# One reciprocal root per token, spread by TensorE; remainders of more weight tiles by the adding DMA; one room each for the mix buffers

## The chip, the cores and the metric

The kernel runs on one core of one Trainium2 chip. Its time is the device time of one launch in microseconds (us). The parts of the core named below are TensorE (PE, which multiplies a stationary 128x128 operand with a moving one into a PSUM bank), VectorE (DVE), ScalarE (ACT), GpSimd (POOL) and the sync engine's queue (SP), which issues the plain DMAs. PEld is the load of PE's stationary operand. POOL issues the DMAs that add to what stands in SBUF.

## The reference

Two layers, each with three residual steps on h, which is 512 tokens x 1024 in fp32:

```python
u = rms_norm(h, g_mlp) @ w_ff1                       # 1024 -> 4096
h = h + jnp.square(jax.nn.relu(u)) @ w_ff2           # 4096 -> 1024
gate = jax.nn.sigmoid(rms_norm(h, g_ple) @ w_ple_gate + b_ple_gate)
h = h + gate * (p_i @ w_ple)
```

In front of these stands h + [sparse attention heads || mLSTM heads](rms_norm(h) @ w_in) @ w_out, called the mix below. rms_norm(x, g) is x * rsqrt(mean(x*x) + 1e-6) * g. The reciprocal root is one number per token, so it can be applied after a matrix product.

## The kernel before

h is held transposed: eight tiles `const_1` to `const_8`, each 128 features (partitions) x 512 tokens. So the token runs along the free dimension, and a factor per token must lie in all 128 partitions as a row of 512.

All products are exact to fp32: an operand x is split into `hi` (x rounded to fp32r by an ACT copy) and `lo` (x - hi), and a product is three matmuls (`mm3`): hi*hi, lo*hi, hi*lo. A weight tile (`weight`, line 541 ff.) is 128x1024: a raw load by SP (`raw<-ws`), the ACT copy `hi`, and `lo` in one of two ways. The direct way is one DVE subtraction `lo<-raw,hi`. The adder way (adder=True) is a second ACT copy, of -hi into `lo`, and a DMA issued by POOL that adds the raw tile to it (`lo<-raw`); the raw tile must then stay until that DMA has landed.

`prep` makes the split operands of a norm: for each of the eight tiles of h, ACT squares it, POOL adds the square to a running sum (`acc`), and ACT and DVE make hi and lo of h times the gain. `wide_r` (lines 612-628) then turns `acc` (128x512) into the reciprocal root of each token, in all partitions: an ACT copy, a DVE subtraction, two matmuls 128x512 with a matrix of ones (sum over partitions, tile `ps_tr`), a DVE scale (`s<-ps_tr`), and ten DVE operations of `rsqrt` on 128x512. It is called twice in a layer: in the MLP (lines 1237-1240) and in the gate step, called ple (line 1311). The mix has its own forms: `token_r` (four matmuls 128x1, then rsqrt on 128x4, a token to a partition) and `spread` (lines 630-649), which lays such a 128x4 out as 128x512 by two diagonal tiles and two matmuls with ones.

The MLP has 32 tiles of w_ff1 and 32 of w_ff2 in a layer. The first four of w_ff1 are direct (`ff1`, lines 1252-1256). The other 28 go in 14 pairs (`pair`, `left`, lines 771-801 and 815 ff.) by Strassen's scheme with seven products of 256 columns. `left` loads two raw tiles r1 and r2, and DVE builds from them r3 (the tile `sum`), r1-r2 and so on, in place; ACT and DVE split each. A product adds into PSUM bank x, and DVE or ACT must read x before the next product adds to it. Between the products of a pair stand blocks of w_ff2, whose tiles are adder tiles; so per pair SP loads r1, r2 and two adder tiles. After the MLP the ple step multiplies two tiles of w_ple, then eight tiles of w_ple_gate, all direct.

The order of the work is made by a planner (`Plan`, list scheduling in Python with ranks and costs) and then pinned: each engine's queue is issued in that order, and every recorded operation bears line L390. Buffers live in rooms (line 1338): `s` 62 (128x512), `raw` 4, `sum` 1, `hi` 4, `lo` 4 and so on. A buffer waits until the last user of its room is done, and SP issues in order, so a load that waits for a room holds up those behind it.

Of the kernel before, what the change touches and what calls it, by code (L numbers as in the profile page):

```python
# [401 lines left out]
class Trunk:  # L402
# [209 lines left out]
    def wide_r(self, acc, dim):  # L612

        nc = self.nc
        chain, nc.chain = nc.chain, None
        label, nc.label = nc.label, "norm"
        hi, lo = self.slot([128, S], F32R), self.slot([128, S], F32R)
        nc.scalar.activation(hi, acc, AF.Copy)
        nc.vector.tensor_tensor(lo, acc, hi.bitcast(F32), op=ALU.subtract)
        ps = self.psum("tr")  # L620
        nc.tensor.matmul(ps, self.onesr, hi, start=True, stop=False)
        nc.tensor.matmul(ps, self.onesr, lo, start=False, stop=True)
        nc.chain = chain
        v = self.slot([128, S])
        nc.vector.tensor_scalar(v, ps, 1.0 / dim, EPS, op0=ALU.mult, op1=ALU.add)
        r = self.rsqrt(v, [128, S])
        nc.label = label
        return r

# [112 lines left out]
    def operands(self, xs, forms):  # L742

        H = S // 2
        lower, upper = slice(0, H), slice(H, S)
        out = []
        for j, (t12, t34) in enumerate(forms):
            d, first = {}, self.slot([128, S], F32R)  # L750
# [33 lines left out]
    def left(self, l, i):  # L784
# [5 lines left out]
        r3 = self.slot([128, 1024], F32, "sum")  # L790
# [70 lines left out]
    def mix(self, l):  # L861
# [42 lines left out]
        at = [self.slot([128, GA]) for _ in range(NTB)]  # L904
# [8 lines left out]
        for tb in range(NTB):  # L913
            nc.scalar.activation(at[tb], pss[tb][:, 0:GA], AF.Copy, scale=r[:, tb:tb + 1])
        ks = [at[tb][:, 0:192].split(64) for tb in range(NTB)]
        wi = self.tiny([128, NTB, 8])
        for tb in range(1, NTB):
            nc.vector.tensor_scalar(wi[:, tb], at[tb][:, 320:328], IDX_SCALE, None, op0=ALU.mult)
# [62 lines left out]

        gi, gf = g4(), g4()
        for tb in range(NTB):
            nc.vector.tensor_tensor(gi[:, tb], at[tb][:, 328:332], ct[:, T_I:T_I + 4], op=ALU.add)
            nc.vector.tensor_tensor(gf[:, tb], at[tb][:, 332:336], ct[:, T_F:T_F + 4], op=ALU.add)
# [46 lines left out]
        vx = [self.slot([128, 4, 129]) for _ in range(NTB)]  # L1032
        for tb in range(NTB):
            nc.gpsimd.memset(vx[tb][:, :, 128:129], 1.0)
        rh = self.tiny([128, NTB])
        nc.vector.tensor_scalar(rh, r, 0.5, None, op0=ALU.mult)
        og = []
        for base in (W_V, W_O):
            ps = [self.psum("proj") for _ in range(NTB)]
            for k in range(KD):  # L1040
                if k % 2 == 0:
                    w = self.wtile(l, base + k // 2, adder=True)
                for tb in range(NTB):
                    self.token_step(ps[tb], w, 512, xs[k], k, 2, tb, k == 0, k == KD - 1)
            for tb in range(NTB):
                if base == W_V:
                    nc.scalar.activation(vx[tb][:, :, 0:128], ps[tb].split(128), AF.Copy, scale=r[:, tb:tb + 1])
                else:
                    og.append(self.slot([128, 512]))
                    nc.scalar.activation(og[tb], ps[tb], AF.Tanh, scale=rh[:, tb:tb + 1])  # L1050
# [23 lines left out]
        for qb in range(NTB):  # L1074
# [3 lines left out]
            for h in range(8):  # L1078
# [21 lines left out]
                for sb in range(qb + 1):  # L1100
                    nc.tensor.matmul(po[:, h * 64:(h + 1) * 64], et[:, sb * 128:(sb + 1) * 128],
                                     at[sb][:, 192 + g * 64:256 + g * 64], start=sb == 0, stop=sb == qb)
# [18 lines left out]
        for h in range(4):  # L1121
# [26 lines left out]
            for tb in range(NTB):  # L1148
                for sb in range(tb + 1):
                    c = (tb - sb) * 128  # L1150
                    nc.tensor.matmul(where(tb), ptile[sb][:, c:c + 128], vx[sb][:, h], start=sb == 0, stop=sb == tb)
# [71 lines left out]
    def mlp(self, l):  # L1223
# [28 lines left out]
        def ff1(i, n=1):  # L1252
            for j, ps in enumerate(self.blocks([self.wtile(l, W_FF1 + i + j) for j in range(n)], xs)):
# [41 lines left out]
    def ple(self, l):  # L1295
# [7 lines left out]
        for n0, cnt in ((0, 2), (2, 1), (3, 1), (4, 1), (5, 1), (6, 1), (7, 1)):  # L1303
            ws = [self.wtile(l, W_GATE + n0 + j) for j in range(cnt)]

            last = l == L - 1 and n0 == KD - 1
            for c in (slice(0, S // 2), slice(S // 2, S)) if last else (slice(0, S),):
                pss = self.blocks(ws, [(hi[:, c], lo[:, c]) for hi, lo in xs], c)
                for n, ps in enumerate(pss, n0):
                    if rbc is None:  # L1310
                        rbc = self.wide_r(acc, D)
# [26 lines left out]
ROOMS = {"s": 62, "raw": 4, "sum": 1, "hi": 4, "lo": 4, "tiny": 48, "wide": 16, "m8": 4, "ps": 8}  # L1338
# [85 lines left out]
```

## Time and profile before

| | |
|---|---|
| median of three runs | 1372.84 us (1370.74 to 1373.17) |
| profiled execution | 1370.38 us, span 1368.7 us |
| granted TensorE clock, mean | 0.989 of full |
| busy: PE, PEld | 1320.8 us (97%), 1127.3 us (82%) |
| busy: DVE, ACT, POOL | 960.8 us (70%), 776.5 us (57%), 194.5 us (14%) |
| DMA | 176.37 MB, the 16 engines about half busy |

The span runs from the first to the last recorded instruction; the profiled execution's own time is 1.7 us more. In a row of the timeline the first number is the start in us from the span's start, the second how long the operation (or the run of like operations, xN) took, and the brackets hold the idle time of the engine before it with what ended it. Names of tiles have their numbers cut off in the profile: `s` is any tile of the s rooms, `const` here mostly h. The MLP of layer 0 runs from about 280 to 620 us, its ple step to 690; those of layer 1 from 955 and from 1295 us.

### The profile page before, as it was taken

Reading aid. Unit: us, or ns where it says so; the run is one execution under the profiler, and the core shown is the slowest. Engines: PE = TensorE matmul, PEld = TensorE weight load, DVE = VectorE, ACT = ScalarE, POOL = GpSimd, SP = SyncE. Lnnn points to the kernel's source line nnn. Section 1 sums busy time; section 2 is a strip of 40 time slices with the busy share of each in tenths; the row PEclk is TensorE's granted clock in tenths of the full one; section 3 lists DMA queues with packets and bytes.
Section 4 is the critical chain, followed back from the end, with each engine's and each line's share of the span. In section 5 each row is a group of like instructions: output and inputs, shape, how many; then the busy total and the mean of one; then the engine's idle time right before and its main releaser. Section 6 shows DMA issues by size and latency. Waiting matters only on the chain.

```text
span 1368.7 us, 20039 instructions
## 1 busy us (share of the span) xinstructions
PE 1320.8 (97%) x7344; PEld 1127.3 (82%) x7344; DVE 960.8 (70%) x2066; ACT 776.5 (57%) x1463; POOL 194.5 (14%) x233
## 2 busy tenths in 40 slices
PE   7999989989999999999999999999999999999988
PEld 6877868868988888987897778887888889889877
DVE  7899697596555656547859996957865565756484
ACT  4885685565545455455548956757554536445541
POOL 4221110210001010012113211003000101000110
PEclk9999999999999999999999999999999999999999
DMA  6556630535555555664243677024546555456621
GB/s 205 125 140 169 153 78 2 138 93 159 134 152 140 156 143 144 160 163 129 73 123 77 159 172 163 33 47 108 139 129 163 132 151 149 140 145 164 169 77 62
DMA packets 51075, 176.37 MB, mean 129 GB/s; under 512 B 6048, under 2 KB 6560, under 8 KB 50976
## 3 DMA queue, kind: packets, MB, share of 16 engines
q1 hardware_dynamic: 34848, 116.37, 26.2%
q0 software_dynamic: 16128, 58.73, 23.2%
q8 instruction: 57, 0.93, 0.3%
q14 instruction: 42, 0.34, 0.1%
HBM read 114.25 MB, written 2.10 MB: 85 GB/s over the span
## 4 chain that ended last, share of the span: by engine, by line
PE 60%; DMA 14%; DVE 13%; issue 9%; ACT 3%; SPq 0%; POOL 0%; POOLq 0%; DVEq 0%; ACTq 0%
PE ps_proj L390 51%; DMA raw<-ws 8%; DVE s L390 5%; DMA lo<-raw 5%; PE ps_tr L390 3%; DVE lo L390 3%; PE ps_sc L390 2%; PE ps_po L390 2%; ACT s L390 1%; DVE const L390 1%; DVE tiny L390 1%; PE ps_pn L390 1%; DMA s<-pt 1%; DVE sum L390 1%; ACT hi L390 1%
## 5 line engine op out<-in xcount | busy, mean ns | idle before, releaser
L390 PE MATMUL ps_proj<-s,hi 128*128 128x256 f32 (+1 forms) x3408 | 889.3, 352 | 14.8 <-ACT s L390 5.7
L390 PEld LDWEIGHTS ps_proj<-s,hi 128*128 128x128 f32 x3408 | 594.6, 190 | 108.1 <-DVE s L390 8.2
L390 PE MATMUL ps_proj<-s,lo 128*128 128x256 f32 (+1 forms) x1704 | 593.6, 351 | 2.5 <-DVE lo L390 2.3
L390 PEld LDWEIGHTS ps_proj<-s,lo 128*128 128x128 f32 x1704 | 322.8, 189 | 49.7 <-DVE lo L390 4.9
L390 ACT ACTIVATE hi<-raw 128x1024 fp32r<-128x1024 f32 (+1 forms) x212 | 221.4, 1046 | 194.9 <-PE ps_proj L390 146.4
L390 POOL DMA_DIRECT2D lo<-raw x112 | 96.7, 864 | 907.2 <-ACT lo L390 593.3
L390 ACT ACTIVATE s<-s 128x512 fp32r<-128x512 f32 (+3 forms) x174 | 101.0, 601 | 130.2 <-DVE s L390 111.9
L390 DVE TENSOR_TENSOR const<-const,ps_proj 128x512 f32<-128x512 f32 x160 | 109.3, 683 | 73.7 <-PE ps_proj L390 73.3
L390 DVE TENSOR_TENSOR lo<-raw,hi 128x1024 fp32r<-128x1024 f32 (+1 forms) x99 | 125.3, 1269 | 21.1 <-ACT hi L390 11.9
L390 DVE TENSOR_TENSOR s<-s,s 128x512 fp32r<-128x512 f32 (+2 forms) x140 | 98.7, 727 | 40.7 <-ACT s L390 39.2
L390 ACT ACTIVATE lo<-raw 128x1024 fp32r<-128x1024 f32 x112 | 117.8, 1052 | 11.9 <-PE ps_proj L390 7.7
L390 PE MATMUL ps_proj<-hi,s 128*128 128x512 f32 (+1 forms) x384 | 112.0, 380 | 7.9 <-ACT hi L390 7.1
L390 DVE TENSOR_TENSOR sum<-raw 128x512 f32<-128x512 f32 x28 | 19.4, 692 | 135.9 <-DMA raw<-ws 135.9
L390 PE MATMUL ps_sc<-s,s 128*128 128x384 f32 (+3 forms) x288 | 80.1, 375 | 4.0 <-DVE tiny L390 3.0
L390 PEld LDWEIGHTS ps_proj<-hi,s 128*128 128x128 f32 x384 | 68.8, 192 | 17.2 <-ACT hi L390 7.1
L390 POOL TENSOR_TENSOR s<-s,s 128x512 f32<-128x512 f32 x42 | 59.5, 1416 | 114.3 <-ACT s L390 101.2
L390 ACT ACTIVATE s<-ps_proj 128x256 f32<-128x256 f32 (+1 forms) x104 | 41.7, 415 | 49.2 <-PE ps_proj L390 49.2
L390 PE MATMUL ps_proj<-lo,s 128*128 128x512 f32 (+1 forms) x192 | 65.9, 380 | 0.6 <-DVE lo L390 0.6
L390 ACT ACTIVATE s<-raw 128x512 fp32r<-128x512 f32 x28 | 17.6, 628 | 84.5 <-DVE raw L390 84.5
L390 PEld LDWEIGHTS ps_sc<-s,s 128*128 128x128 f32 x288 | 49.8, 190 | 16.7 <-DVE tiny L390 4.1
L390 DVE SCALAR_TENSOR_TENSOR s<-s,s 128x512 f32<-128x512 f32 (+1 forms) x85 | 50.4, 595 | 6.5 <-ACT s L390 5.0
L390 ACT ACTIVATE s<-ps_tr 128x128 fp32r<-128x128 f32 (+2 forms) x170 | 41.0, 317 | 21.4 <-PE ps_tr L390 20.9
(139 smaller groups left out, 1457.4 us busy)
## 6 DMA issues: line engine op xcount, KB each, us to landing
raw<-ws SPq DMA_DIRECT2D x204, 512.0 KB, 3.7
lo<-raw POOLq DMA_DIRECT2D x112, 512.0 KB, 5.3
raw<-wa SPq DMA_DIRECT2D x8, 336.0 KB, 3.3
const<-xt SPq DMA_DIRECT2D x8, 256.0 KB, 5.1
s<-pt SPq DMA_DIRECT2D x8, 256.0 KB, 4.7
out<-const SPq DMA_DIRECT2D x7, 256.0 KB, 2.0
const<-ct SPq DMA_DIRECT2D x2, 132.0 KB, 4.8
out<-const SPq DMA_DIRECT2D x2, 128.0 KB, 1.7
```

The source lines that it names most:

```text
L390: ins = getattr(getattr(nc, e), method)(*[value(x) for x in args], **{k: value(x) for k, x in kw.items()}).ins
```

## The change

It has four parts. `wide_r` goes; the MLP and the gate call `spread(token_r(acc))`: four matmuls 128x1 instead of the wide ones, rsqrt on 128x4, then a DVE cast and a subtraction on 128x4, two DVE products 128x512, two matmuls 128x512, and one ACT copy out of PSUM. The first four w_ff1 tiles of each layer and the first three w_ple_gate tiles become adder tiles (14 tiles in all). The rooms change: `raw` 4 to 3, `s` 62 to 60, `sum` goes, and one room each comes for `at` (the mix's key projections as one tile for all tokens, later r3 of the pairs) and `vx` (the mLSTM's values, later a part of the pairs' right operands). With `at` and `vx` whole, ten small operations per layer become three, and one memset stands for four.

```diff
-    def wide_r(self, acc, dim):
 ...
-        out = []
+        out, firsts = [], self.slot([128, KD // 2, S], F32R, "vx")
...
-        r3 = self.slot([128, 1024], F32, "sum")
+        r3 = self.slot([128, 1024], F32, "at")
...
-        at = [self.slot([128, GA]) for _ in range(NTB)]
+        at = self.slot([128, NTB, GA], tag="at")
...
-        for tb in range(1, NTB):
-            nc.vector.tensor_scalar(wi[:, tb], at[tb][:, 320:328], IDX_SCALE, None, op0=ALU.mult)
+        nc.vector.tensor_scalar(wi, at[:, :, 320:328], IDX_SCALE, None, op0=ALU.mult)
...
-        vx = [self.slot([128, 4, 129]) for _ in range(NTB)]
+        vx = self.slot([128, NTB, 4, 129], tag="vx")
...
-                state["r"] = self.wide_r(acc, D)
+                state["r"] = self.spread(self.token_r(acc, D))
...
-            for j, ps in enumerate(self.blocks([self.wtile(l, W_FF1 + i + j) for j in range(n)], xs)):
+            for j, ps in enumerate(self.blocks([self.wtile(l, W_FF1 + i + j, adder=True) for j in range(n)], xs)):
...
-            ws = [self.wtile(l, W_GATE + n0 + j) for j in range(cnt)]
+            ws = [self.wtile(l, W_GATE + n0 + j, adder=n0 < 3) for j in range(cnt)]
...
-                        rbc = self.wide_r(acc, D)
+                        rbc = self.spread(self.token_r(acc, D))
...
-ROOMS = {"s": 62, "raw": 4, "sum": 1, "hi": 4, "lo": 4, "tiny": 48, "wide": 16, "m8": 4, "ps": 8}
+ROOMS = {"s": 60, "raw": 3, "hi": 4, "lo": 4, "at": 1, "vx": 1, "tiny": 48, "wide": 16, "m8": 4, "ps": 8}
```

The planner orders every queue anew. Three places matter below. The first is SP's queue in the pairs of layer 0's MLP, with the semaphores that each load waits for. A wait on DMASW is one for an adder's landing, a wait on DVE alone one for DVE's last use of the room. Before, raw_1002 and raw_1003 are r1 and r2 of a pair, raw_1032 and raw_1033 those of the next:

```order
L390 DMA raw_1017_3851<-ws 128x1024 [waits DMAHW3_49,DMASW4_49,Activation_49]
L390 DMA raw_1002_3883<-ws 128x1024 [waits DMAHW4_49,DVE_49]
L390 DMA raw_1003_3978<-ws 128x1024 [waits DMAHW6_49,DMASW5_49,Activation_49]
L390 DMA raw_1023_4032<-ws 128x1024 [waits DMAHW5_49,DVE_49]
L390 DMA raw_1047_4054<-ws 128x1024 [waits DMAHW7_49,DMASW6_49,Activation_49]
L390 DMA raw_1032_4086<-ws 128x1024 [waits DMAHW0_49,DVE_49]
L390 DMA raw_1033_4153<-ws 128x1024 [waits DMAHW2_49,DMASW7_49,Activation_49]
```

Now, with raw_997 and raw_998 as the same pair's r1 and r2, and raw_1027 and raw_1028 as the next pair's:

```order
L390 DMA raw_1012_3892<-ws 128x1024 [waits DMAHW4_49,DVE_49]
L390 DMA raw_997_3957<-ws 128x1024 [waits DMAHW6_49,DMASW1_49,Activation_49]
L390 DMA raw_998_4014<-ws 128x1024 [waits DMAHW5_49,DVE_49]
L390 DMA raw_1018_4036<-ws 128x1024 [waits DMAHW7_49,DMASW2_49,Activation_49]
L390 DMA raw_1042_4089<-ws 128x1024 [waits DMAHW0_49,DVE_49]
L390 DMA raw_1027_4138<-ws 128x1024 [waits DMAHW2_49,DMASW3_49,Activation_49]
L390 DMA raw_1028_4217<-ws 128x1024 [waits DMAHW1_49,DVE_49]
```

The loads stand in the same order, but the wait for an adder has moved from r2 to r1: the adder tile in front of the pair (raw_993 before, raw_988 now, the same weights) gave its room to r2 and gives it to r1.

The second place is DVE's queue at the same pair. Before, ps_proj_985 is the pair's bank x, and sum_1004 the r3 of the next pair:

```order
L390 TENSOR_TENSOR s_983_3961<-s_983_3961,ps_proj_985_3946 128x256
L390 TENSOR_TENSOR const_1_63<-const_1_63,ps_proj_990_3966 128x512
L390 TENSOR_TENSOR sum_1004_3999<-raw_1003_3978 128x512
L390 TENSOR_TENSOR sum_1004_3999<-sum_1004_3999,raw_1002_3883 128x512
L390 TENSOR_TENSOR lo_982_4022<-raw_973_3747,hi_981_3968 128x1024
L390 TENSOR_TENSOR const_2_95<-const_2_95,ps_proj_992_4018 128x512
L390 TENSOR_TENSOR lo_1006_4049<-raw_1002_3883,hi_1005_4020 128x1024
L390 TENSOR_TENSOR s_984_4005<-s_984_4005,ps_proj_985_3946 128x256
```

Now bank x is ps_proj_980, and r3 is at_999:

```order
L390 TENSOR_TENSOR s_978_3948<-s_978_3948,ps_proj_980_3932 128x256
L390 TENSOR_TENSOR const_1_63<-const_1_63,ps_proj_985_3951 128x512
L390 TENSOR_TENSOR lo_977_4004<-raw_968_3811,hi_976_3953 128x1024
L390 TENSOR_TENSOR const_2_89<-const_2_89,ps_proj_987_4000 128x512
L390 TENSOR_TENSOR lo_1001_4031<-raw_997_3957,hi_1000_4002 128x1024
L390 TENSOR_TENSOR s_979_3988<-s_979_3988,ps_proj_980_3932 128x256
L390 TENSOR_TENSOR at_999_4046<-raw_998_4014 128x512
```

The operation that reads r2 (`sum_1004<-raw_1003`, now `at_999<-raw_998`) stood ahead of the second reading of bank x and stands behind it now.

The third place is ACT's queue at the start of layer 1's ple step. Before, hi_2760 is the second tile of w_ple, hi_2822 and hi_2825 are the first two gate tiles, and the rows that read const are the squares and gains of `prep`:

```order
L390 ACTIVATE s_2801_13242<-const_4_132,const_21_360 128x512
L390 ACTIVATE s_2803_13249<-const_4_132 128x512
L390 ACTIVATE s_2805_13268<-const_5_152,const_21_360 128x512
L390 ACTIVATE s_2807_13273<-const_5_152 128x512
L390 ACTIVATE hi_2760_13281<-raw_2759_13206 128x1024
L390 ACTIVATE s_2809_13291<-const_6_165,const_21_360 128x512
L390 ACTIVATE s_2811_13297<-const_6_165 128x512
L390 ACTIVATE s_2813_13317<-const_7_187,const_21_360 128x512
L390 ACTIVATE s_2815_13321<-const_7_187 128x512
L390 ACTIVATE hi_2825_13331<-raw_2824_13127 128x1024
L390 ACTIVATE s_2817_13342<-const_8_214,const_21_360 128x512
L390 ACTIVATE s_2819_13350<-const_8_214 128x512
```

Now hi_2754 is that tile of w_ple, and the gate tiles are hi_2816 and hi_2819, with lo_2820 the adder's copy:

```order
L390 ACTIVATE hi_2754_13244<-raw_2753_13208 128x1024
L390 ACTIVATE s_2797_13251<-const_4_116 128x512
L390 ACTIVATE s_2795_13258<-const_4_116,const_21_285 128x512
L390 ACTIVATE s_2799_13265<-const_5_136,const_21_285 128x512
L390 ACTIVATE s_2801_13272<-const_5_136 128x512
L390 ACTIVATE hi_2816_13282<-raw_2815_13129 128x1024
L390 ACTIVATE s_2803_13293<-const_6_149,const_21_285 128x512
L390 ACTIVATE s_2805_13300<-const_6_149 128x512
L390 ACTIVATE s_2807_13319<-const_7_171,const_21_285 128x512
L390 ACTIVATE s_2809_13324<-const_7_171 128x512
L390 ACTIVATE hi_2819_13334<-raw_2818_13154 128x1024
L390 ACTIVATE lo_2820_13345<-raw_2818_13154 128x1024
```

The copy of w_ple's tile has moved from behind the squares of const_5 to ahead of those of const_4; and two copies, not one, now stand ahead of the square of const_8, which is ACT's next row.

## Rows read from the trace of the kernel before

**Rows 1.** The page: busy time, share of the span, instructions.
```profile
PE 1320.8 (97%) x7344; PEld 1127.3 (82%) x7344; DVE 960.8 (70%) x2066; ACT 776.5 (57%) x1463; POOL 194.5 (14%) x233
```
**Rows 2.** Windows: span, width, busy of each engine, then PE clock, DMA share.
```profile
275.00:300.00 25.00, 21.05 (x79) 15.93 (x78) 23.35 (x35) 14.74 (x26) 5.68 (x4) 0.86 0.36 103
625.00:650.00 25.00, 22.67 (x89) 17.07 (x88) 21.09 (x23) 15.30 (x24) 8.20 (x6) 0.93 0.32 104
400.00:425.00 25.00, 24.37 (x148) 21.42 (x147) 13.32 (x21) 11.97 (x18) 1.72 (x2) 1.00 0.57 155
...
1150.00:1175.00 25.00, 24.23 (x152) 21.51 (x152) 14.37 (x22) 12.64 (x18) 1.72 (x2) 1.00 0.51 138
...
1300.00:1325.00 25.00, 21.29 (x83) 16.79 (x82) 20.21 (x21) 14.08 (x23) 6.87 (x6) 0.86 0.33 106
```
**Rows 3.** Timeline of PE: the wait in a pair, and the product S3*T3.
```profile
445.42 0.76 PE L390 MATMUL ps_proj<-s,s 128*128 128x256 f32 x5
452.21 0.51 PE L390 MATMUL ps_proj<-s,hi 128*128 128x256 f32 x2 [0.63 <-DVE s L390]
```
**Rows 4.** Timeline of DVE in the same pair.
```profile
423.96 0.69 DVE L390 TENSOR_TENSOR sum<-raw 128x512 f32<-128x512 f32 x1 [5.14 <-DMA raw<-ws]
447.54 0.69 DVE L390 TENSOR_TENSOR sum<-raw 128x512 f32<-128x512 f32 x1 [6.86 <-DMA raw<-ws]
451.74 0.41 DVE L390 TENSOR_TENSOR s<-s,ps_proj 128x256 f32<-128x256 f32 x1
```
**Rows 5.** Timeline of SP, POOL and ACT in the same pair.
```profile
431.35 11.87 SPq L390 DMA_DIRECT2D raw<-ws  x2
438.34 0.86 POOL L390 DMA_DIRECT2D lo<-raw  x1 [17.53 <-ACT s L390]
437.00 1.04 ACT L390 ACTIVATE lo<-raw 128x1024 fp32r<-128x1024 f32 x1
442.72 1.06 ACT L390 ACTIVATE hi<-raw 128x1024 fp32r<-128x1024 f32 x1 [0.92 <-PE ps_proj L390]
443.68 0.36 ACT L390 ACTIVATE s<-ps_proj 128x256 f32<-128x256 f32 x1
```
**Rows 6.** The page: DMA issues, KB each, median us to landing.
```profile
raw<-ws SPq DMA_DIRECT2D x204, 512.0 KB, 3.7
lo<-raw POOLq DMA_DIRECT2D x112, 512.0 KB, 5.3
```
**Rows 7.** Groups by form: busy, mean ns of one, idle before.
```profile
L390 DVE TENSOR_TENSOR lo<-raw,hi 128x1024 fp32r<-128x1024 f32 x91 | 115.8, 1275 | 20.6 <-ACT hi L390 11.4 <-PE ps_proj L390 8.4
L390 PE MATMUL ps_tr<-const,s 128*128 128x1 f32 x32 | 3.9, 243 | 0.0
```
**Rows 8.** Timeline of PE and POOL where layer 0's MLP begins.
```profile
283.35 0.69 PE L390 MATMUL ps_proj<-s,hi 128*128 128x512 f32 x1 [2.58 <-ACT s L390]
285.18 0.80 PE L390 MATMUL ps_tr<-s,const 128*128 128x512 f32 x1 [1.14 <-ACT s L390]
286.20 0.79 PE L390 MATMUL ps_proj<-s,hi 128*128 128x512 f32 x1 [0.23 <-DVE s L390]
282.92 1.54 POOL L390 TENSOR_TENSOR s<-s,s 128x512 f32<-128x512 f32 x1 [2.01 <-ACT s L390]
```
**Rows 9.** Timeline where layer 1's ple step begins: PE, ACT, DVE, POOL.
```profile
1305.82 3.78 PE L390 MATMUL ps_proj<-s,hi 128*128 128x512 f32 x8 [3.71 <-ACT hi L390]
1315.64 0.40 PE L390 MATMUL ps_tr<-s,const 128*128 128x512 f32 x1
1304.73 1.04 ACT L390 ACTIVATE hi<-raw 128x1024 fp32r<-128x1024 f32 x1
1299.53 1.73 DVE L390 TENSOR_TENSOR lo<-raw,hi 128x1024 fp32r<-128x1024 f32 x1
1311.06 0.68 DVE L390 TENSOR_TENSOR const<-const,ps_proj 128x512 f32<-128x512 f32 x1
1313.16 1.40 POOL L390 TENSOR_TENSOR s<-s,s 128x512 f32<-128x512 f32 x1 [0.84 <-ACT s L390]
```

More of the change, by code (lines that the diff above doesn't have):

```diff
@@ L610, in token_r @@
         return r
-    def wide_r(self, acc, dim):
[L614 to L628, printed above, removed]
     def spread(self, r):
@@ L747, in operands @@
         lower, upper = slice(0, H), slice(H, S)
-        out = []
+        out, firsts = [], self.slot([128, KD // 2, S], F32R, "vx")
         for j, (t12, t34) in enumerate(forms):
-            d, first = {}, self.slot([128, S], F32R)
+            d, first = {}, firsts[:, j]
             for part, c in zip(xs[2 * j], (lower, upper)):
@@ L913, in mix @@
         for tb in range(NTB):
-            nc.scalar.activation(at[tb], pss[tb][:, 0:GA], AF.Copy, scale=r[:, tb:tb + 1])
-        ks = [at[tb][:, 0:192].split(64) for tb in range(NTB)]
+            nc.scalar.activation(at[:, tb], pss[tb][:, 0:GA], AF.Copy, scale=r[:, tb:tb + 1])
+        ks = [at[:, tb, 0:192].split(64) for tb in range(NTB)]
         wi = self.tiny([128, NTB, 8])
-        for tb in range(1, NTB):
-            nc.vector.tensor_scalar(wi[:, tb], at[tb][:, 320:328], IDX_SCALE, None, op0=ALU.mult)
+        nc.vector.tensor_scalar(wi, at[:, :, 320:328], IDX_SCALE, None, op0=ALU.mult)
         self.headnorm(ks, 3, ct[:, T_K:T_K + 192], True)
@@ L980, in g4, with bias4 @@
             return self.tiny([128, NTB, 4])
+        def bias4(col):
+            return ct[:, col:col + 4].unsqueeze(1).broadcast_to([128, NTB, 4])
         gi, gf = g4(), g4()
-        for tb in range(NTB):
-            nc.vector.tensor_tensor(gi[:, tb], at[tb][:, 328:332], ct[:, T_I:T_I + 4], op=ALU.add)
-            nc.vector.tensor_tensor(gf[:, tb], at[tb][:, 332:336], ct[:, T_F:T_F + 4], op=ALU.add)
+        nc.vector.tensor_tensor(gi, at[:, :, 328:332], bias4(T_I), op=ALU.add)
+        nc.vector.tensor_tensor(gf, at[:, :, 332:336], bias4(T_F), op=ALU.add)
         nab, z, y, y2, lp, lf = g4(), g4(), g4(), g4(), g4(), g4()
@@ L1031, in mix @@
         nc.chain = "rows"
-        vx = [self.slot([128, 4, 129]) for _ in range(NTB)]
-        for tb in range(NTB):
-            nc.gpsimd.memset(vx[tb][:, :, 128:129], 1.0)
+        vx = self.slot([128, NTB, 4, 129], tag="vx")
         rh = self.tiny([128, NTB])
-        nc.vector.tensor_scalar(rh, r, 0.5, None, op0=ALU.mult)
+        nc.hold, held = nc.vector.tensor_scalar(rh, r, 0.5, None, op0=ALU.mult), nc.hold
+        nc.gpsimd.memset(vx[:, :, :, 128:129], 1.0)
+        nc.hold = held
         og = []
@@ L1046, in mix @@
                 if base == W_V:
-                    nc.scalar.activation(vx[tb][:, :, 0:128], ps[tb].split(128), AF.Copy, scale=r[:, tb:tb + 1])
+                    nc.scalar.activation(vx[:, tb, :, 0:128], ps[tb].split(128), AF.Copy, scale=r[:, tb:tb + 1])
                 else:
@@ L1101, in mix @@
                     nc.tensor.matmul(po[:, h * 64:(h + 1) * 64], et[:, sb * 128:(sb + 1) * 128],
-                                     at[sb][:, 192 + g * 64:256 + g * 64], start=sb == 0, stop=sb == qb)
+                                     at[:, sb, 192 + g * 64:256 + g * 64], start=sb == 0, stop=sb == qb)
             rs = self.tiny([128, 8])
@@ L1150, in mix @@
                     c = (tb - sb) * 128
-                    nc.tensor.matmul(where(tb), ptile[sb][:, c:c + 128], vx[sb][:, h], start=sb == 0, stop=sb == tb)
+                    nc.tensor.matmul(where(tb), ptile[sb][:, c:c + 128], vx[:, sb, h], start=sb == 0, stop=sb == tb)
             nc.chain = None
```

## The prediction

> **What bounds the kernel now.** The page's busy times come first: PE is busy 1320.8 of 1368.7 us, DVE 70% [rows 1]. PE alone sets the pace; whatever the change takes from DVE counts only where PE waits for DVE. PE is idle for 1368.7 - 1320.8 = 47.9 us, and that with PE's own work is all that can move. Then the windows of 25 us, to see where those 47.9 us lie. There are two kinds of place [rows 2]. At the starts of the MLP and ple steps (the windows at 275, 625 and 1300 us; the one at 950 is like the one at 275) PE is busy for 21 to 23 us, and the granted clock falls to 0.86 or 0.93. A mean of 0.86 over 25 us is 25 x 0.14 / 0.5 = 7 us at the lower level (1.2 GHz), 0.93 is 3.5 us; there the work takes twice as long, so each such fall costs up to half of those 7 or 3.5 us, beside the idle time. In the pairs most windows read 25.00, but seven show 24.23 to 24.63 at full clock. The rest lies at the start, the end and in the mix. Last, the timeline of PE in those places says for whom it waits.
>
> The profiled execution took 1370.38 us (span and 1.7 us around it), 2.46 less than the median of 1372.84. I work out a difference and add it to the median. A measurement of this kernel can tell 0.2%, 2.75 us, from no change.
>
> **The change part by part.**
>
> The pairs. PE waits 0.63 us at 452.21, released by DVE [rows 3]. DVE's operation ahead of that is the second reading of bank x at 451.74, late because DVE had stood 6.86 us at r2's landing until 447.54 and then worked off what was queued behind [rows 4]. r2 was late because its load stood at the head of SP's queue: the two issues that start at 431.35 end at 443.22, the second having waited for the adder issued by POOL at 438.34 [rows 5]. Seven such windows miss 25 - 24.37 = 0.63 to 0.77 us each, 4.7 us together [rows 2]. In the new order the reading of bank x stands ahead of r2's first use, so this wait goes whatever r2 does.
>
> What is late next? r1: it now waits for the adder. Its copy stands in ACT's queue at 442.72, and behind it the reading of bank x at 443.68, which ends at 444.04 [rows 5] and which PE needs for S3*T3 at 445.42 [rows 3]. So r1 may be 1.4 us late and cost nothing. When does it land? From the adder's issue at 438.34 to the load's issue (443.22 less about 0.3) were 4.5 us; a load lands after 3.7 us [rows 6]. With the adder where it was, r1 would land at 442.9 + 3.7 = 446.6, 3.9 us after its place and 2.5 beyond the slack, in every second pair. But the adder's copy at 437.00 is itself late: DVE stood at the r2 of the pair before until 423.96 [rows 4], and DVE and ACT worked off what had piled up. Without that wait of 5.14 us the copy is bound by PE's products of the pair before. A matmul of 512 columns takes PE 0.23 us (eight took 3.78 at the lower clock [rows 9]), one of 256 half of that. From the start of S3*T3 PE does three products and a block of w_ff2, 36 x 0.115 + 12 x 0.23 = 6.9 us; then come a relu on DVE and four ACT operations of about 0.6 us on half the copy's width, so the copy stands some 10 us after S3*T3. A whole pair is 84 x 0.115 + 48 x 0.23 = 20.7 us, with its small gaps some 21.5; the S3*T3 before that of 445.42 began near 423.9. That puts the copy near 433.5, 3.5 us earlier. r1 then lands near 443.1, 0.4 us late and inside the slack by 1.0 us. In the pairs between, the new order has the adder's copy ahead of the four relu and square operations, so r1 has some 3 us more. I take a gain of 4.0 of the 4.7 us. Range: -4.7 to +7 (0.5 us beyond the slack in 14 of the 28 pairs).
>
> The norms in the MLP. wide_r's two matmuls of 128x512 are replaced by spread's two, and the four matmuls 128x1 come on top: 8 records of 3.9/32 = 0.12 us, 1.0 us a call [rows 7]. PE idles 2.58 + 1.14 + 0.23 = 3.95 us at the MLP's start, and takes off at 286.20 [rows 8]. Now the four small matmuls stand ahead of the last steps and wait for POOL's last addition, which ended at 284.46 [rows 8]. One direct subtraction of 1.28 us [rows 7] leaves DVE's queue there, and by the new order two shorter operations come in; I put the addition 0.5 us earlier. PE is free at 284.0 + 1.0 = 285.0 instead of 286.2, with the three matmuls of 128x512 still to do that before ran in its gaps (0.7 us): a gain of about 0.4 us, from -1.5 to +1 each, since the clock falls either way. The ten operations of rsqrt shrink from 512 to 4 columns; nobody on PE waited for them, so that gives nothing. Two layers: -0.8.
>
> The norm of layer 0's gate is as above, with 25 - 22.67 = 2.3 us of idle in its window [rows 2]: -0.6 (-2.5 to +1).
>
> The norm of layer 1's gate. PE idles 3.71 us until 1305.82 for w_ple's copy, which ACT does at 1304.73 behind squares that wait for DVE [rows 9]. That copy now stands ahead of five squares and gains and could run some 5 us earlier, so this wait goes. What is late next is w_ple's remainder on DVE. By the new order two tiles' gains and additions, some 2 us each, lie between it and const_8, which puts its end near 1306.0; PE starts at 1305.82 - 3.71 = 1302.1, runs ten matmuls of 0.23 us to 1304.4 and waits 1.6 us. Then come 20 matmuls (4.6 us) to 1310.6, and there the four small matmuls want the sum of squares. Before, POOL's last addition ended at 1314.56, and the ps_tr at 1315.64 hardly waited [rows 9]. Now const_8 is ready some 1 us before its 1311.74 (a subtraction of 1.73 us [rows 9] leaves DVE's queue, waits for ACT stay), but two ACT copies (1.04 each [rows 9]) stand ahead of its square where one stood, and POOL issues an adder (0.86 [rows 5]) ahead of the last addition (1.40): 1313.5 if each follows at once, 1314.6 if nothing is gained. So PE waits 2.9 to 4.0 us there. Idle is 4.5 to 5.6 instead of 3.7 us, and the fall of the clock, which came behind the 3.71 us, comes behind the second wait: I take +1.0 (-2.5 to +4).
>
> Here a rule bears on the row. DVE's subtraction of 1299.53 took 1.73 us instead of the mean of 1.275 [rows 7, 9], while POOL was adding. The Trainium skill, "SBUF — State Buffer", section "SBUF: two separate sides", says that DVE and GpSimd share one pair of ports as an exclusive lock: a DVE operation with two SBUF operands and a GpSimd operation that reads SBUF block each other for the whole instruction. The trace shows 0.45 us more, less than the 1.40 us of an addition [rows 9], so it agrees in sign only. By that rule each of the two subtractions that leave this stretch could give POOL's chain an addition's length, and the term would be about -2 instead of +1; I stay with the rows.
>
> The start. With three raw rooms the fourth load must wait for the first tile's remainder on DVE, and the loads behind it too; PE is bound there by DVE anyway. Between nothing and one subtraction (1.28 [rows 7]) I take +0.3. The merged small operations lie on DVE beside PE's work and count nothing. The mix is planned anew: its scores and transposes stand some ten blocks earlier among the filling matmuls in layer 0 and a few later in layer 1. The trace has no price for that. Of the 47.9 us some 29 are left when the pairs (4.7) and the four starts (3.95 twice, 2.3, 3.7) are taken off; they lie in the two mixes, the start and the end. I take 0, and a seventh of them, 4 us, to either side.
>
> Sum: -4.0 - 0.8 - 0.6 + 1.0 + 0.3 + 0 = -4.1 us, 1372.84 - 4.1 = 1368.7 us.
>
> **The rivals.**
>
> A. r1 comes late and PE stalls in the pairs. For it: the margin of 1.0 us rests on 4.5 us for the adder where the median is 5.3 [rows 6], and r1's load now runs beside r2's. Against it: SP's order is the same and the pairs between have more room. It decides from a landing of r1 1.4 us after ACT's place for it. With 0.5 us beyond, in 14 pairs, the pairs give +7 instead of -4: 1372.84 + 6.9 = 1379.7 us, slower.
>
> B. Nothing that can be measured. What goes at 1305 and in the pairs comes back as other waits: PE's total is bound by its own matmuls, which grow by 4 x 1.0 us, and DVE's freed time is off the path. For it: the transitions are chains through ACT, DVE and POOL in which no step vanishes. Against it: the 0.63 us waits have one plain cause. The pairs then give -2, the small matmuls and the gates +2: 1372.8 us.
>
> C. The transitions shrink as well. If the sums of squares end 1.5 us earlier at each of the four places and two of the clock's falls of 3.5 us (1.7 us each) stay away, that is another -4 x 1.0 - 3.4: -4.1 - 7.4 = -11.5, 1361.3 us. For it: DVE loses 14 subtractions, which at POOL's additions cost 1.7 us [rows 9]. Against it: the copies that come in on ACT stand in the same chain.
>
> **How the numbers follow.** My forecast 0.50, A 0.25, B 0.15, C 0.10. The forecast's own range is 1364 to 1373, wide by the mix. The range for 8 in 10 reaches toward C and A: 1362 to 1380 us. Faster by over 2.75 us: 0.65 of the forecast (0.33), all of C, some of B: 0.45. Slower: 0.07 of the forecast, 0.75 of A, some of B: 0.24. Within: 0.31.
>
> **What would show it.** In the profile after: no wait of PE for DVE in the pairs, and windows there of 25.00; DVE's wait at r3's first operation short. Rival A would show as a wait of ACT's hi copy for the DMA raw, and PE's S3*T3 waiting for ACT. At layer 1's ple step the 3.71 us wait for hi should be gone and two waits stand in its place, for DVE's lo and, at the 128x1 matmuls, for POOL's sum. The forecast is wrong if the pairs' windows fall below 24.3, or if the mix moves by more than 4 us.

## The result and the profile after

The changed kernel takes 1388.21 us (median of 4 runs, 1387.41 to 1390.31) against 1372.3 of the kernel before (4 runs): 1.2% slower, ratio 1.012, 95% interval [1.0102, 1.0137]. The forecast was 1368.7 us, faster; the time also lies outside the range of 1362 to 1380. The side is rival A's, and in the pairs so is the mechanism; the loss of 15.9 us is over twice A's 6.9. The profiled execution has a span of 1385.7 us at a mean clock of 0.986, so 17.0 us more than before.

The page after, line for line with [rows 1]:
```profile
PE 1317.3 (95%) x7376; PEld 1132.2 (82%) x7376; DVE 920.9 (66%) x2042; ACT 790.5 (57%) x1483; POOL 208.7 (15%) x241
```
DVE's busy time fell by 40 us, as the diff says. PE's fell by 3.5 us, though it has 32 matmuls more. Idle time of PE rose from 47.9 to 68.4 us: the change lost it all in waits.

Windows of 25 us after, columns as in [rows 2]:
```profile
350.00:375.00 25.00, 22.95 (x147) 20.53 (x146) 13.39 (x21) 11.98 (x19) 2.58 (x3) 1.00 0.58 142
400.00:425.00 25.00, 22.95 (x147) 20.55 (x146) 13.18 (x20) 11.06 (x17) 1.72 (x2) 1.00 0.62 156
...
1300.00:1325.00 25.00, 21.27 (x90) 16.87 (x89) 11.38 (x14) 13.24 (x19) 7.03 (x6) 0.99 0.64 155
```
The forecast called itself wrong if a pair's window fell below 24.3; here is 22.95, at full clock, so PE stands still for 2.05 us, in one piece by the rows below. The window at 1300 has the idle time it had, at a higher clock.

To see where 17.0 us lie I cut the span at PE's rows: the starts of the first and the last 256-column matmul of each layer's pairs, and of the last matmul of all. The end of what came before is the start of the next stretch.

| us | start, mix 0, to pairs | pairs 0 | ple 0, mix 1, to pairs | pairs 1 | ple 1, end |
|---|---|---|---|---|---|
| before | 306.3 | 296.2 | 376.5 | 296.8 | 87.7 |
| after | 306.2 | 301.2 | 381.6 | 304.0 | 87.5 |
| difference | -0.1 | +5.0 | +5.1 | +7.2 | -0.2 |

PE's timeline in the pairs after, each a wait at S3*T3, the product of [rows 3]:
```profile
362.03 1.69 PE L390 MATMUL ps_proj<-s,s 128*128 128x256 f32 x12 [2.05 <-ACT s L390]
406.43 1.69 PE L390 MATMUL ps_proj<-s,s 128*128 128x256 f32 x12 [2.05 <-ACT s L390]
450.80 1.69 PE L390 MATMUL ps_proj<-s,s 128*128 128x256 f32 x12 [1.93 <-ACT s L390]
495.18 1.67 PE L390 MATMUL ps_proj<-s,s 128*128 128x256 f32 x12 [2.10 <-ACT s L390]
...
1253.65 0.39 PE L390 MATMUL ps_proj<-s,lo 128*128 128x256 f32 x1 [2.29 <-DVE lo L390]
```
They come every 44.4 us, in every second pair of the first half; layer 1 has four of 2.04 to 2.08 too, the last row and one of 0.34. That is 19.0 us. The waits for DVE that stood there before (six of 0.62 or 0.63 and three of 0.16 to 0.42, 4.6 us) are gone: +14.4, against +12.2 in the table. The 2.2 us between the two are not accounted for.

The same pair on ACT, with SP's and POOL's part (answers to [rows 5]):
```profile
435.11 1.06 ACT L390 ACTIVATE hi<-at 128x1024 fp32r<-128x1024 f32 x1 [2.14 <-PE ps_proj L390]
436.07 2.18 ACT L390 ACTIVATE s<-s 128x512 fp32r<-128x512 f32 x4
438.16 1.05 ACT L390 ACTIVATE lo<-raw 128x1024 fp32r<-128x1024 f32 x1
...
449.42 1.06 ACT L390 ACTIVATE hi<-raw 128x1024 fp32r<-128x1024 f32 x1 [4.31 <-DMA raw<-ws]
450.38 0.37 ACT L390 ACTIVATE s<-ps_proj 128x256 f32<-128x256 f32 x1
```
```profile
439.49 0.86 POOL L390 DMA_DIRECT2D lo<-raw  x1 [17.01 <-ACT lo L390]
442.71 0.86 POOL L390 DMA_DIRECT2D lo<-raw  x1 [2.36 <-ACT lo L390]
```
```profile
444.09 3.69 SPq L390 DMA_DIRECT2D raw<-ws  x2
```
Read from the bottom of the chain: the adder's copy ends at 439.21 and POOL issues the adder at 439.49; 4.6 us after that, at 444.09, SP issues r1's load; ACT's copy of r1 stands 4.31 us for it until 449.42; behind that copy stands the reading of bank x at 450.38, and PE goes on 0.42 later. In the profile's DMA rows for this issue the landing is:
```profile
raw<-ws SPq DMA_DIRECT2D x1, 512.0 KB, 5.2
```
The list of waits after shows the same over the whole span (total, times, longest):
```profile
ACT hi L390 <- DMA raw<-ws: 74.5, 21, 8.0
DVE at L390 <- DMA raw<-ws: 36.1, 10, 8.3
```
In the list of before, DVE's wait is
```profile
DVE sum L390 <- DMA raw<-ws: 135.9, 26, 7.1
```
DVE's wait for r2 fell from 135.9 us to 36.1. It did not vanish: ACT now waits for r1, and where DVE's wait had cost PE 0.63 us, ACT's costs 2.05.

PE in the mix, layer 0's and layer 1's:
```profile
98.79 0.70 PE L390 MATMUL ps_tr<-const,s_sp 128*128 128x128 f32 x4 [3.27 <-ACT vx L390]
...
780.26 0.75 PE L390 MATMUL ps_tr<-const,s_sp 128*128 128x128 f32 x4 [3.67 <-ACT vx L390]
```
On ACT in layer 0, the operation of `vx` at 98.06 is behind a weight tile's copy:
```profile
96.16 1.06 ACT L390 ACTIVATE lo<-raw 128x1024 fp32r<-128x1024 f32 x1 [2.70 <-DMA raw<-ws]
97.12 1.04 ACT L390 ACTIVATE hi<-raw 128x1024 fp32r<-128x1024 f32 x1
98.06 1.82 ACT L390 ACTIVATE vx<-ps_proj,tiny 128x512 f32<-128x512 f32 x3
```
The first of these copies had waited for its load and, in ACT's fixed order, held up what stood behind it.

### The profile page after: what moved, and what is told of

The parts are those of the page before. It is cut to its first block, busy times and chain, and to the rows that moved or that the text cites. A ratio compares the mean times of both kernels' runs of the same rounds, so it can differ in the third digit from the quotient of the medians.

```text
span 1385.7 us, 20123 instructions
## 1 busy us (share of the span) xinstructions
PE 1317.3 (95%) x7376; PEld 1132.2 (82%) x7376; DVE 920.9 (66%) x2042; ACT 790.5 (57%) x1483; POOL 208.7 (15%) x241
## 4 chain that ended last, share of the span: by engine, by line
PE 63%; DMA 12%; DVE 10%; issue 7%; ACT 6%; POOL 1%; SPq 0%; POOLq 0%; DVEq 0%; ACTq 0%
PE ps_proj L390 54%; DMA raw<-ws 7%; DVE s L390 6%; DMA lo<-raw 4%; PE ps_tr L390 3%; PE ps_sc L390 3%; ACT s L390 2%; PE ps_po L390 2%; ACT hi L390 2%; PE ps_pn L390 1%; DMA s<-pt 1%; DVE tiny L390 1%; ACT lo L390 1%; ACT s_idx L390 1%; DVE const L390 1%
## 5 line engine op out<-in xcount | busy, mean ns | idle before, releaser
L390 PE MATMUL ps_proj<-s,hi 128*128 128x512 f32 (+1 forms) x3184 | 846.0, 355 | 7.3 <-DVE const L390 3.7
L390 PEld LDWEIGHTS ps_proj<-s,hi 128*128 128x128 f32 x3184 | 559.5, 189 | 94.5 <-DVE s L390 4.8
L390 PE MATMUL ps_proj<-s,lo 128*128 128x512 f32 (+1 forms) x1592 | 560.2, 355 | 2.6 <-DVE lo L390 2.6
L390 PEld LDWEIGHTS ps_proj<-s,lo 128*128 128x128 f32 x1592 | 301.6, 189 | 46.8 <-DVE lo L390 3.6
L390 DVE TENSOR_TENSOR lo<-raw,hi 128x1024 fp32r<-128x1024 f32 (+1 forms) x85 | 103.9, 1224 | 94.2 <-ACT hi L390 52.1
L390 ACT ACTIVATE lo<-raw 128x1024 fp32r<-128x1024 f32 x126 | 132.4, 1051 | 16.1 <-PE ps_proj L390 7.7
L390 ACT ACTIVATE s<-s 128x512 fp32r<-128x512 f32 (+2 forms) x154 | 90.1, 619 | 70.6 <-DVE s L390 37.9
L390 PE MATMUL ps_sc<-s,s 128*128 128x256 f32 (+3 forms) x288 | 85.3, 382 | 5.2 <-DVE s_t L390 4.6
L390 PE MATMUL ps_proj<-s,s 128*128 128x256 f32 x336 | 45.2, 284 | 16.4 <-ACT s L390 16.4
L390 PEld LDWEIGHTS ps_proj<-s,s 128*128 128x128 f32 x336 | 43.1, 189 | 21.6 <-ACT s L390 19.8
```

Of the source, the lines that this page charges most:

```text
L390: ins = getattr(getattr(nc, e), method)(*[value(x) for x in args], **{k: value(x) for k, x in kw.items()}).ins
```

## The experiments

My theory after these rows: three raw rooms are the whole loss. Every load waits for a user of its room one tile sooner, and ACT's and DVE's fixed orders pass each late load on to PE. The rivals: the new norm (four small matmuls and a longer chain), the adder tiles, and the new order of the mix. The time of the kernel before, on the same chips, was 1372.62 (runs 1 to 4), 1370.11 (5 to 8), 1371.14 (9 to 12) and 1370.23 us (13, 14).

**1. The order of after, untouched, with a fourth raw room.** After the planning, a function deals the rooms out again in the order of issue; no instruction moves on any engine. `s` gets 58 rooms (57 are held at most).
```diff
+        self.again({"s": 58, "raw": 4})
+    def again(self, rooms):
+        ...
+        free = {k: list(range(n)) for k, n in rooms.items()}
+        for op in self.order:
+            for b in op.new:
+                if b.room in free:
+                    b.place = free[b.room].pop(0)
+            ...        (b's place goes back to the end of the list after b's last user)
```


> The changed kernel with its order on every engine untouched; only the places are dealt out again, raw tiles over four rooms instead of three and s tiles over 58 instead of 60, so that r1 waits for DVE and r2 for the adder again. Theory 1 (three raw rooms put r1 behind an adder's landing): the waits of 2.05 us for ACT at S3*T3, nine in all with the one of 2.29 us, go, the pairs fall from 301.2 and 304.0 us to some 294 to 297 each, the copies of w tiles in the mix come sooner too, and the time is 1369 to 1376 us. Rival (the added adder tiles and their ACT copies, or the new norm, are what costs): the pairs stay over 300 us and the time is above 1384 us.

Measured: 1332.86 us, ratio 0.9722 [0.9702, 0.9741]; 55.4 us less than after, with no instruction moved, by one raw room (and `s` dealt out again). The time is 36 us below the range that I expected: the theory had the pairs' waits right and missed what the room is worth outside them (run 12). The page of this run, and its ACT in the pair that answers to 450.80:
```profile
PE 1303.7 (98%) x7376; PEld 1128.3 (85%) x7376; DVE 920.1 (69%) x2042; ACT 792.3 (59%) x1483; POOL 210.2 (16%) x241
```
```profile
422.00 1.04 ACT L407 ACTIVATE lo<-raw 128x1024 fp32r<-128x1024 f32 x1
...
430.12 1.06 ACT L407 ACTIVATE hi<-raw 128x1024 fp32r<-128x1024 f32 x1 [0.93 <-PE ps_proj L407]
431.09 0.37 ACT L407 ACTIVATE s<-ps_proj 128x256 f32<-128x256 f32 x1
```
```profile
432.82 1.59 PE L407 MATMUL ps_proj<-s,s 128*128 128x256 f32 x12
```
The adder's copy stands 10.8 us ahead of S3*T3, as far as in after (448.87, where PE was ready, less 438.16 is 10.7). But r1 waits for another room now, and its copy waits 0.93 us for PE instead of 4.31 for a load. No wait of PE is left in the pairs, nor behind them to the end. The new norm's wait stands here undisturbed: PE waits for POOL's sum at the four small matmuls of the MLP,
```profile
273.03 1.87 PE L407 MATMUL ps_tr<-const,s 128*128 128x1 f32 x8 [2.53 <-POOL s L407]
```

**2. The whole change, planned anew for four raw rooms.**
```diff
-ROOMS = {"s": 60, "raw": 3, ...
+ROOMS = {"s": 58, "raw": 4, ...
```


> The changed kernel planned anew with four raw rooms and 58 s rooms. Theory 1: no wait for the DMA raw in front of ACT's hi in the pairs, 1366 to 1374 us, within 4 us of the run with the order pinned. Rival: 1384 us or more, as the changed kernel. If the order matters as much as the rooms, the two runs differ by more than 5 us.

Measured: 1355.48 us, 0.9881 [0.9856, 0.9905]. A planner that knows of the fourth room uses it up: 22.6 us slower than run 1, whose order was made for three. Its list of waits has before's wait for r2 back:
```profile
DVE at L390 <- DMA raw<-ws: 147.8, 28, 7.5
ACT hi L390 <- DMA raw<-ws: 2.1, 2, 1.7
```
and PE waits 0.61 or 0.62 us for DVE at six places in the pairs, as before. So ACT's wait for r1 went, as expected, but the two runs are not within 4 us, and the time is 10 us below the range of theory 1. Between kernels that are each planned for the rooms they have, the change without the loss of the room is worth about -17 us, and the room 1388.2 - 1355.5 = +33. Both figures hold the luck of a new order.

**3. The new norm alone** in the kernel before (old rooms, direct tiles).
```diff
-                state["r"] = self.wide_r(acc, D)
+                state["r"] = self.spread(self.token_r(acc, D))
```


> The kernel before with only the norms changed (spread of token_r in place of wide_r), planned anew, four raw rooms, no new adder tiles. Theory 1: the pairs are as before (296 to 297 us) and the time is within 4 us of before. A rival that the norm itself costs: PE waits some 3 us for DVE in front of the spread's matmuls at each gate, and the time is 3 to 8 us above before.

Measured: 1376.97 us, 1.0047 [1.0032, 1.0061]: 4.4 us above before, just beyond theory 1 and inside the rival's range. In its trace PE waits 1.98 us for DVE ahead of the spread's matmuls in layer 0's gate, and not at all in layer 1's.

**4. The 14 adder tiles alone** in the kernel before.
```diff
-            ... [self.wtile(l, W_FF1 + i + j) for j in range(n)]
+            ... [self.wtile(l, W_FF1 + i + j, adder=True) for j in range(n)]
-            ws = [self.wtile(l, W_GATE + n0 + j) ...
+            ws = [self.wtile(l, W_GATE + n0 + j, adder=n0 < 3) ...
```


> The kernel before with only the 14 tiles turned into adder tiles, planned anew, four raw rooms, wide_r as before. Theory 1: the pairs are as before and the time is within 4 us of before. The rival that the adder tiles cost (their ACT copies and POOL issues stand in the chain of the sum of squares): the starts of the MLP and the gate grow by 1 to 3 us each, 1376 to 1384 us.

Measured: 1371.68 us, 0.9991 [0.9975, 1.0008], nothing. Runs 3 and 4 leave +4 and -1 us to these two parts, the second no more than noise.

**5. The kernel before, its order pinned, with a fifth raw room** (and 60 of `s`): is it the number of rooms, or slack against the plan?
```diff
+        self.again({"s": 60, "raw": 5})
```


> The kernel before with its order on every engine untouched, raw tiles dealt over five rooms instead of four (s tiles over 60 instead of 62). Theory 2 (what counts is that the rooms that are there are one more than the order was planned for, so that a landing that is later than planned stops nobody): the waits of DVE for r2 (135.9 us in the kernel before) nearly go, PE's waits in the pairs and at the ple steps too, and the time falls by 20 to 45 us to 1328 to 1352 us. Rival (the gain of the pinned run comes from the change's other parts): 1366 to 1375 us, only the 4.7 us of the pairs go.

Measured: 1354.08 us, 0.9877 [0.9858, 0.9896], 16 us below before and 2 above the range of theory 2. No wait of PE is left in the pairs; the rival is out.

**6. The kernel before, planned for three raw rooms and run with its four.**
```diff
-ROOMS = {"s": 62, "raw": 4, "sum": 1, ...
+ROOMS = {"s": 62, "raw": 3, "sum": 1, ...
+        self.again({"s": 62, "raw": 4})
```


> The kernel before planned for three raw rooms, and that order run with four; nothing else of the change. Theory 2: also 20 to 45 us below before, 1328 to 1352 us, without any of the change's parts. Rival: within 6 us of before (1366 to 1378 us).

Measured: 1351.1 us, 0.9853 [0.9835, 0.9872]. With the rooms it always had, the kernel before is 19 us faster in an order that was planned for one fewer. So a room beyond the plan paid at both numbers tried, three and four. Run 1 is another 18 us below this, and those are not explained by slack.

Why the plan has no slack can in part be read in the planner. It gives the raw room of an adder tile back 0.2 us after the 1.1 us that it reckons for the adder's issue (`HOP` and `cost`), and reckons 2.4 us from a load's issue to its use. In the trace after, an adder lands 5.0 us after its issue and a load after 3.6 (medians). So the plan counts on rooms that are not free yet. Whether an order planned with the measured times would still want a spare room was not tried.

**7. Run 1 with `wide_r` back** (the old norm, planned so), and **8. run 1 with the 14 tiles direct**: the diffs of 3 and 4 turned round.

> The changed kernel planned for three raw rooms and run with four, as the pinned run of 1332.9 us, but with wide_r in the MLP and the gate as before. If the new norm is worth something where no room is short: 1335 to 1345 us. If it is off the path: within 3 us of 1332.9. Planned anew, so 5 us either way could be the order.

> The same, but with the new norm kept and the 14 tiles direct again (DVE's subtraction in place of the adder). If the adder tiles are worth something: 1335 to 1345 us, with DVE late at the starts of the MLP and the gate. If not: within 3 us of 1332.9.

Measured: 1330.15 us, 0.9703 [0.9687, 0.9718], and 1334.74 us, 0.9734 [0.9719, 0.9749]. Against run 1 the new norm costs 2.7 us and the adder tiles give 1.9, the same signs as in 3 and 4, and no larger than what another order may do. Run 7 has the lowest median of all and beats both kernels; its interval overlaps those of runs 1 and 9.

**9 and 10. The rooms alone** (`at`, `vx`, merged small operations; old norm, direct tiles), planned for three raw rooms: 9 run with four, 10 the same order run with three.

> Of the change only the rooms (at, vx, r3 in at, the merged small operations), with wide_r and the direct tiles of before; planned for three raw rooms, run with four. Theory 3 (the changed rooms of the mix give what is left between the runs of 1351 us with the old rooms and of 1330 to 1335 us): 1329 to 1337 us, with the stretch up to the first pair near 294 us. Rival (the norm or the adders, one of which was in each of the last two runs, gave it): 1345 to 1353 us.

> The same order run with the three raw rooms that it was planned for, so only the rooms part of the change, as changed. Theory 1 (three raw rooms are the whole cause of the slower kernel): 1380 to 1392 us, the pairs over 300 us each. Rival (three rooms hurt only together with the 14 more adder tiles or the new norm): 1365 to 1375 us.

**11. The norm and the adder tiles alone** with the old rooms, planned for three raw rooms, run with four.

> The new norm and the 14 adder tiles with the old rooms of the mix (s, sum), planned for three raw rooms and run with four. Theory 3: within 5 us of the run with the kernel before planned so, 1346 to 1356 us, with the stretch up to the first pair near 305 us. Rival: 1330 to 1338 us.

Measured: 1332.93 us (9), 0.9715 [0.9697, 0.9733]; 1383.21 us (10), 1.0077 [1.0051, 1.0102]; 1352.59 us (11), 0.9858 [0.9835, 0.9881]. 9 and 10 show the room's price without the norm and the adder tiles: 50 us. The 18 us that slack left open are with `at`, `vx` and the merged operations: 9 has them and is at run 1's time, 11 has not and is at run 6's. By the table's cuts they lie in the two mixes: start 295.1 in 9 against 306.0 in 11, ple 0 and mix 1 365.8 against 374.6; the pairs and the end differ by under 1 us.

**12. The order of after; the fourth raw room only for tiles that are loaded in the MLPs.** Where do the 55 us lie?
```diff
+                    here = [p for p in free[b.room] if b.room != "raw" or p < 3 or op.stage in (1, 4)]
+                    b.place = here[0]
```


> The changed kernel with its order untouched; s over 58 rooms, and a fourth raw room that only the MLP's tiles may take, three everywhere else. Theory 1: the pairs fall to 291 to 294 us each as in the run with four everywhere, and the rest stays as in the changed kernel (306, 381 and 87 us) apart from the tiles that the ple step and the mix find loaded sooner at its edges: 1360 to 1368 us. Rival (the pairs' waits come from a delay that starts in the mix or the ple step): the pairs stay over 298 us, 1380 us and more.

Measured: 1356.96 us, 0.989 [0.9869, 0.9911]. By the same cuts:

| us | start | pairs 0 | ple 0, mix 1 | pairs 1 | ple 1, end |
|---|---|---|---|---|---|
| after | 306.2 | 301.2 | 381.6 | 304.0 | 87.5 |
| run 12 | 305.8 | 291.4 | 378.9 | 290.5 | 81.3 |
| run 1 | 295.5 | 291.4 | 367.7 | 290.5 | 81.3 |

The pairs are run 1's in both layers, 9.8 and 13.5 us less than after; no wait of PE is left in either. The end goes with them, and the time is 3 us below the range expected. SP issues the loads of `pt` (p_i, for the ple step)
```profile
1273.60 1.98 SPq L409 DMA_DIRECT2D s<-pt  x2
```
7.0 us after the start of the pairs' last matmul, where after had
```profile
1304.15 0.90 SPq L390 DMA_DIRECT2D s<-pt  x2
```
11.2 us behind it. They land after 5.7 us instead of 8.9, and ACT stands 2.29 us for them instead of 9.19. The mixes stay nearly as in after, with the same wait:
```profile
98.88 0.72 PE L409 MATMUL ps_tr<-const,s_sp 128*128 128x128 f32 x4 [3.30 <-ACT vx L409]
```
In run 1 that row waits 0.49 us. This run is also the control for the new deal of the rooms: here `s` has run 1's 58 rooms, dealt out by the same function, and the mixes with three raw rooms gain 0.4 and 2.7 us of run 1's 10.7 and 13.9. So in the mixes it is the fourth raw room that pays, and not the dealing; in the pairs the waits that went were waits for loads.

**13 and 14. Which half of the rooms part gives the mixes' 18 us?** Run 9 with less room for `s` in planning (13), and run 9 with the small operations and memsets for each token block apart again (14).
```diff
-ROOMS = {"s": 60, "raw": 3, ...
+ROOMS = {"s": 54, "raw": 3, ...
```
```diff
-        nc.vector.tensor_scalar(wi, at[:, :, 320:328], IDX_SCALE, None, op0=ALU.mult)
+        for tb in range(1, NTB):
+            nc.vector.tensor_scalar(wi[:, tb], at[:, tb, 320:328], IDX_SCALE, None, op0=ALU.mult)
 ...
```


> The rooms part alone (run of 1332.9 us), planned with 54 s rooms instead of 60, still run with 58, and raw 3 run with 4. Before, 62 s rooms held the four at and four vx tiles too, which leaves 54 for the rest. Theory 3a (the mix gained because at and vx no longer take s rooms, so that more of its work can start early): the stretch up to the first pair returns to 303 to 307 us and the time to 1345 to 1355 us. Rival 3b (the merged small operations give it): within 4 us of 1332.9.

> The rooms part alone with 60 s rooms, but the ten small operations and the four memsets of a layer apart again (per token block, as in the kernel before). Theory 3a: within 4 us of 1332.9. Rival 3b: the stretch up to the first pair near 305 us, 1345 to 1355 us.

Measured: 1347.86 us, 0.9836 [0.9812, 0.986], and 1352.76 us, 0.987 [0.9843, 0.9896]: run 13 loses most of the 18 us and run 14 all of them. Run 14's PE waits for `vx` in the mix 2.93 us, where run 9's waits 0.50:
```profile
94.96 0.79 PE L407 MATMUL ps_proj<-hi,s 128*128 128x512 f32 x1 [2.93 <-ACT vx L407]
```
13 fits theory 3a and 14 fits its rival. So neither half holds the gain alone, and which piece of the planned order in the mix does was not settled: each of these edits also made the planner lay out the mix anew.

## Why the prediction was wrong, step by step

**The pairs (forecast -4.0, found +12.2).** That the wait for r2 goes, that r1 then waits for the adder, and where PE would feel it, held row by row. What failed is the step "r1 then lands near 443.1, 0.4 us late and inside the slack by 1.0 us". Its three lengths, against the pair at 450.80, where PE was ready for S3*T3 at 448.87:

| | forecast | found |
|---|---|---|
| adder's copy ahead of S3*T3 | 445.42 - 433.5 = 11.9 | 448.87 - 438.16 = 10.7 |
| adder's copy to the load's issue | 442.9 - 437.0 = 5.9 | 444.09 - 438.16 = 5.9 |
| landing | 3.7 (median) | 5.2 |

The copy is 1.2 us nearer. It stood 10.5 us behind the S3*T3 before (at 427.62) instead of 9.6, and that S3*T3 was 21.25 us ahead instead of 21.5. ACT's copy into `hi` ahead of it waited 2.14 us for PE to give up a `hi` room, and I had counted the four operations but not that wait. The landing is 1.5 us longer: a median over 204 loads was used for one that runs beside an adder, issued at 442.71, and in its last 1.8 us beside SP's next load. 1.2 + 1.5 = 2.7 us against a margin of 1.0 makes 1.7 us, and PE waited 1.93. The working compared a difference of two estimates with 1.0 us, while each of them was open by more than that. Rival A priced 0.5 us in 14 pairs; it was about 2.05 us in eight. Run 1 shows the other side of the same place: with a fourth room r1 does not wait for the adder at all. My theory "three raw rooms are the whole loss" is too strong in the mix, where the rooms of `at` and `vx` bring a gain that the lost room hides, and for the norms below. One reading of the rows before was off as well: the seven windows run from 24.14 to 24.63, and miss 0.37 to 0.86 us each; their sum of 4.7 us stands.

**Start +0.3 and mix 0 (found -0.1 for the first stretch).** The sum came near by luck: two terms cancel. The price of three rooms at the start was put at one DVE subtraction; runs 9 and 10 show 308.4 - 295.1 = 13 us there for the first stretch. And "I take 0" for the mix left out what the changed rooms give its order, about -11 by 9 against 11. Both are parts of the same stretch that the trace of before could not show apart.

**The norms in the MLP (-0.8).** The small matmuls did wait for POOL's sum, 2.53 us, as said; with the rest of the transition the whole is +2.7 us over four norms (run 1 against 7) or +4.4 (run 3), not a gain. Each of these compares two orders, so the size is rough. No gain from the ten shortened operations shows, as said.

**Layer 0's gate (-0.6, found about +2.4).** The transition's waits were 2.3 us and are 1.59 for POOL at 645.28 and
```profile
654.36 0.47 PE L390 MATMUL ps_tr<-s,const 128*128 128x512 f32 x1 [3.14 <-DVE s L390]
```
The cause is on DVE, whose chain of small operations starts late:
```profile
646.37 0.16 DVE L390 TENSOR_SCALAR tiny<-ps_tr 128x4 f32<-128x4 f32 x1 [0.58 <-PE ps_tr L390]
650.14 1.23 DVE L390 TENSOR_TENSOR lo<-raw,hi 128x1024 fp32r<-128x1024 f32 x1 [3.61 <-ACT hi L390]
651.28 0.16 DVE L390 TENSOR_SCALAR tiny<-tiny 128x4 int32<-128x4 int32 x1
```
A weight's remainder stands between the first and second operation of the root, and waits 3.61 us for ACT's copy. Shorter operations in a chain are no gain where the queue puts a stranger into it. In the whole stretch PE's idle time grew from 12.3 to 17.3 us, beside the table's +5.1; mix 1 has the other large ones, 3.67 us behind `vx` and 2.78 for DVE at 853.05.

**Layer 1's gate (+1.0, found -0.2 for the stretch).** W_PLE's copy is no longer what PE waits for, as said. The two waits that I put in its place are one, of the old size:
```profile
1323.67 1.57 PE L390 MATMUL ps_proj<-s,hi 128*128 128x512 f32 x4 [3.73 <-DVE const L390]
```
Ahead of it DVE stood 10.94 us until 1313.70 behind ACT's copy of `pt`, whose load SP issued behind ten weight loads at 1304.15, and then had a queue to work off. With the pairs' room back (run 12) ACT has `pt` 7 us earlier, counted from the end of the pairs, and PE has no wait at all after its second pairs. I had not followed SP's queue there.

POOL's additions lengthened that queue too. Two of DVE's operations in it stand beside two of them:
```profile
1319.96 3.05 DVE L390 SCALAR_TENSOR_TENSOR s<-const,const,s 128x512 fp32r<-128x512 f32 x2 [1.36 <-ACT s L390]
```
```profile
1319.47 1.26 POOL L390 TENSOR_TENSOR s<-s,s 128x512 f32<-128x512 f32 x1
1321.20 1.26 POOL L390 TENSOR_TENSOR s<-s,s 128x512 f32<-128x512 f32 x1 [0.47 <-ACT s L390]
```
With no addition beside them, two such operations take 1.5 us. In run 12 the same two take 3.11 us and cost PE nothing, so it is the late `pt` that lets them be felt. The prediction read its own row of this too weakly. The addition beside DVE's subtraction of 1299.53 was
```profile
1298.64 1.53 POOL L390 TENSOR_TENSOR s<-s,s 128x512 f32<-128x512 f32 x1 [0.84 <-ACT s L390]
```
and only its last 0.64 us, until 1300.17, fell into the subtraction, which took 0.5 us more than the 1.22 of those with no addition beside them. So 0.64 us, and not the whole 1.40, is what the row must be held against. The Trainium skill, "SBUF — State Buffer", section "SBUF: two separate sides", lets whichever of the two starts first keep the shared ports for its whole instruction. The trace agrees with that nearly in size, not in sign only.

## What to carry to other kernels

Before a buffer is taken from a ring of loads, follow one whole turn of the ring (last user, issue, landing, first use) in the fixed queues; an order that this planner made for n rooms had no slack with n, and the same order run with one more gained 16 to 55 us here. Hold a planner's times against the trace, above all how long it keeps a room. Margins of a microsecond that rest on a median landing are no margins: take the landing under the load that will run beside it. Test parts of a change with the scarce buffer given back, since its loss may hide that the rest is a gain: here, each version planned anew, +33 us hid -17.

## What was not expected of the hardware

A 512 KB load landed in 5.2 us, beside an accumulating DMA issued 1.4 us earlier and another load, against a median of 3.6 us in the same run. The accumulating DMA alone does not explain it. By the issues and landings in the trace after, the loads that ran for at least 1 us beside an accumulating DMA and no other had a median of 3.6 us (52 loads), those beside another plain DMA alone 3.8 (67), those beside both 5.2 (36), and the rest 3.5 (49). PE's median pace in the pairs from one matmul's start to the next was the same in all runs (0.23 us for 512 columns, 0.12 for 256), so that the differences told here are nearly all wait and clock. PE's busy time fell with the waits, too: 1317.3 us in after and 1303.7 in run 1 for the same 7376 instructions, at a mean granted clock of 0.986 and 0.992.
